# A new table of priorities, and a new split of sums between GpSimd and VectorE, in the two mixers of a hybrid decoder step

## The chip, the core and the metric

The program runs on one core of one Trainium2 chip. Its engines work side by side, each through its own instructions in their order: TensorE (PE in the profile) multiplies, VectorE (DVE), ScalarE (ACT) and GpSimd (POOL) do the elementwise work, SyncE (SP) issues the transfers. The metric is the device time of one execution in microseconds (us).

## The reference, cut to what matters

512 prompt tokens behind 16 learned ones, and 8 sample tokens, go through two layers. All is float32.

```python
x = x + 0.5 * _swiglu(_rmsnorm(x, norm_ffn1), ffn1_w_in, ffn1_w_out)
h, wkv, shift, conv = _mixer(_rmsnorm(x, norm_mix), ...)
x = x + h
x = x + 0.5 * _swiglu(_rmsnorm(x, norm_ffn2), ffn2_w_in, ffn2_w_out)

def _mixer(xn, ...):
    ps, pc, pg = split(xn @ w_in)                 # shifted, convolution and gate columns
    ...
    S = S * w_t + (S @ a_t) b_t + v_t k_t         # RWKV-7 state, token by token, 16 heads of 64
    y = S @ r_t
    ...
    m = sigmoid(gate_a) * y_a + sigmoid(gate_b) * (gb * conv(gc * hc))
    return m @ w_o, ...
```

## The kernel before, in words

The order on each engine is not the program's: class `Sched` records every operation (`add`), and `flush` runs a small model of the five engines and issues, on each engine in turn, the ready operation of lowest `prio`. A priority is the place in the program less `boost`. The model is flushed five times: for the FFN (swiglu) stretch of layer 0, its mixer, the FFN stretch between the layers, the mixer of layer 1, and the last FFN stretch. This case touches what the two mixers (`mixer`, called "mixer 0" and "mixer 1" here) hand to it.

A product of two float32 numbers is made of three products of rounded halves: a weight tile `raw` comes by a transfer of SP, ScalarE writes its upper half `hi`, VectorE the rest `lo` (`load_split`), and `mm3` issues for each 128 rows hi by xh, hi by xl, lo by xh, each for two halves of the columns (268, or 262 and 260 in layer 1). A projection (`proj`) is 48 such matmuls into one of two `acc` accumulators in PSUM. They are called column matmuls here.

A mixer has eight pairs of heads. Pair p goes through `stage_k(p)` (projections k and r, decay, key norm: `kq` is split into `kqh` and `kql` for the matmuls `wn`; the chunk matrix `mv`, its products `wg`; the inverse `Xinv` on GpSimd with `pr`), `stage_v(p)` (projection v, `wv`, `wg`, `wp`, and the bonus `bv`), `chain(p)` (11 chunks of 48 tokens that follow each other), `gnorm(p)` (group norm, with the split `yl`) and `stage_m(p)`. One step of a chain is PE, VectorE, ... in turn: `cq<-mv,sd` (PE), `rh` (VectorE), `cq<-cst,rh` (PE), `rd` (VectorE), `cq<-rd,Yd` (PE), `ud` (ScalarE), `cq<-GR,ud` (PE), `sx` and `P` (VectorE), `cq<-cst,sx` (PE), `sd` (VectorE). What PE has between these five matmuls are column matmuls of the next pairs and of `gated_parts`, the 40 gated projections with their elementwise work; `fill(p, i)` says how many of them are recorded at which place, by the list `gated`.

`sample` updates the state of the 8 sample rows in eight steps of 512 elements, on GpSimd and VectorE: `s1` (t<-s,VB), a sum, `sw` (s<-s,VB), `s2`, `s2a`, `s3`, `s3a`, `s4`, a sum. Its result `ys` goes into every column of the merged tile, so the first W_o product (`acc<-mh`) can't start without it.

The table `MIX` has one entry for each mixer: `boost` by stage (k, v, c chain, g gnorm, f gated parts, m, s sample, i inverse, w merge, e eviction of a projection, h weight loads), `gated`, `same` (how far ScalarE may put off an operation that needs another function table), and `vector`: the sums and products named there go to VectorE, the others to GpSimd:

```python
E = lambda n: V if n in opt['vector'] else G
...
E('kql').tensor_tensor(out=kql[:, :L], in0=kq[:, :L], in1=kqh[:, :L].bitcast(F32), op=ALU.subtract)
```

The model already counts one port that GpSimd and VectorE's operations with two SBUF inputs share (`o.port`, with `SHARE = 0.7`); that part is the same in both kernels. All recorded operations stand at line 273 of the profile, so rows are told apart by tile names.

Of the kernel before, what the change touches and what calls it, by code (L numbers as in the profile page):

```python
# [38 lines left out]
RW = C + D  # L39
NH = 16  # L40

MIX = [dict(boost={'k': 600, 'v': 2000, 'c': 2000, 'g': -1500, 'f': -1000, 'm': -1000, 's': -1000, 'i': 2000, 'w': -6000, 'e': 0, 'h': 0},
            ka=4, gated=[0, 2, 0, 0, 0, 1, 1, 1, 0, 0, 2, 1, 0, 1, 1, 2, 0, 1, 2, 1, 0, 0, 0, 1, 2, 2, 0, 0, 2, 1, 0, 0],
            same=3000, inv=(),
            vector=('bv', 'ka', 'kh', 'kql', 'kt', 'm', 'mb', 'rk', 'rnip', 'rt', 's1', 's3a', 'sl', 'u', 'yl', 'zg')),
       dict(boost={'k': 1500, 'v': -1000, 'c': 2000, 'g': 100, 'f': -3000, 'm': -50, 's': 1000, 'i': 1500, 'w': 50, 'e': -2000, 'h': -2000},
            ka=4, gated=[0, 3, 0, 0, 1, 0, 0, 1, 1, 0, 2, 2, 1, 0, 0, 1, 0, 0, 1, 4, 1, 0, 1, 0, 1, 1, 0, 1, 1, 1, 0, 0],
            same=0, inv=(),
            vector=('bv', 'kh', 'kql', 'kt', 'm', 'mb', 'rk', 'rt', 's3a', 'sl', 'u', 'yl', 'zg'))]
LATE = 4.0  # L50
SHARE = 0.7
FIRST = -300
# [307 lines left out]
class Build:  # L360
# [423 lines left out]
    def mixer(self, l, xh, xl, mD):  # L784
        tc, nc, io, cst, R = self.tc, self.nc, self.io, self.cst, self.R
        V, G, A, T, S = nc.vector, nc.gpsimd, nc.scalar, nc.tensor, nc.sync
        pc = lambda n, i: self.pcol(l, n, i)
        opt = MIX[l]
        nc.same = opt['same']
# [659 lines left out]
    def wo(self, l, X, mh, ml):  # L1449

        nc, n, ka = self.nc, self.n, MIX[l]['ka']
        for j in range(KD):
# [166 lines left out]
```

## Time and profile before

| | us |
|---|---|
| median of three runs | 2955.64 (2954.28 to 2958.29) |
| the profiled execution, its own time | 2957.18 |
| its span, first to last instruction | 2955.4 |
| PE busy | 2873.6 |
| VectorE busy | 2135.9 |
| ScalarE busy | 1362.6 |
| GpSimd busy | 587.7 |

The profile gives for each stretch of time how long each engine was busy, and the share of full speed that PE's clock was granted. A row of the timeline has the start, the length, the engine and operation, output<-inputs and shape; in brackets stands how long the engine sat idle before it, and what ended that.

### The profile page before, as it was taken

How to read it: one execution, taken by the hardware profiler on the slowest of the kernel's cores; microseconds unless marked ns; L12 is line 12 of the kernel's file. 1: busy time of each engine (PE TensorE's matmuls, PEld its weight loads, DVE VectorE, ACT ScalarE, POOL GpSimd, SP SyncE). 2: the span in 40 equal slices, each digit the busy share in tenths (PEclk: the TensorE clock that was granted, in tenths of full speed). 3: DMA queues.
4: the chain of work that ended last, by engine and by line, in shares of the span. 5: the costliest groups of instructions: out<-in, count | busy, mean ns of one | idle time of the engine just before them, and what ended most of it. 6: DMA issues, size and time to landing. Idle time of an engine off the chain costs nothing.

```text
span 2955.4 us, 57453 instructions
## 1 busy us (share of the span) xinstructions
PE 2873.6 (97%) x23026; PEld 2811.0 (95%) x23026; DVE 2135.9 (72%) x3995; ACT 1362.6 (46%) x2284; POOL 587.7 (20%) x1120
## 2 busy tenths in 40 slices
PE   8999999999999899999999999999999999999998
PEld 8999999999999899999999999999899998899997
DVE  8677767677776968676687766667766768687775
ACT  5444454344444245444454444535454442554444
POOL 1000026222342800000100001343430428100001
PEclk9999999999999989999999999999999999999999
DMA  3223323232323362323323333232232234623332
GB/s 133 93 96 98 112 87 92 74 86 83 87 64 99 130 207 87 104 90 104 108 71 101 100 94 116 90 96 78 62 84 75 62 103 139 214 79 108 96 102 80
DMA packets 219516, 294.22 MB, mean 100 GB/s; under 512 B 119824, under 2 KB 128784, under 8 KB 219248
## 3 DMA queue, kind: packets, MB, share of 16 engines
q1 hardware_dynamic: 219248, 290.54, 32.0%
q8 instruction: 181, 2.97, 0.4%
q14 instruction: 87, 0.71, 0.1%
HBM read 256.38 MB, written 34.10 MB: 98 GB/s over the span
## 4 chain that ended last, share of the span: by engine, by line
PE 86%; DVE 6%; ACT 2%; DMA 2%; issue 2%; POOL 1%; SPq 0%; DVEq 0%; ACTq 0%; POOLq 0%
PE acc L273 26%; PE a L273 17%; PE x L273 13%; PE y L273 7%; PE cq L273 5%; PE wg L273 3%; PE au L273 3%; PE z L273 3%; PE ag L273 3%; PE w L273 2%; DVE lo L273 2%; PE wp L273 2%; DMA raw<-in_f_in 1%; ACT hi L273 1%; POOL t L273 1%
## 5 line engine op out<-in xcount | busy, mean ns | idle before, releaser
L273 ACT ACTIVATE hi<-raw 128x1024 fp32r<-128x1024 f32 (+4 forms) x460 | 388.5, 845 | 488.6 <-PE acc L273 190.4
L273 DVE TENSOR_TENSOR lo<-raw,hi 128x1024 fp32r<-128x1024 f32 (+4 forms) x460 | 449.3, 978 | 58.0 <-ACT hi L273 52.2
L273 PE MATMUL acc<-xh,hi 128*128 128x268 f32 (+1 forms) x2112 | 481.3, 301 | 6.8 <-ACT sig L273 2.2
L273 PE MATMUL acc<-xh,lo 128*128 128x268 f32 (+1 forms) x2112 | 482.3, 301 | 5.5 <-DVE lo L273 5.4
L273 PE MATMUL acc<-xl,hi 128*128 128x268 f32 (+1 forms) x2112 | 478.2, 299 | 0.0
L273 PEld LDWEIGHTS acc<-xh,hi 128*128 128x128 f32 x2112 | 343.6, 192 | 12.5 <-ACT sig L273 3.3
L273 PEld LDWEIGHTS acc<-xh,lo 128*128 128x128 f32 x2112 | 343.6, 192 | 10.9 <-DVE lo L273 8.8
L273 PEld LDWEIGHTS acc<-xl,hi 128*128 128x128 f32 x2112 | 343.1, 191 | 1.1
L273 PE MATMUL a<-hh,lo 128*128 128x268 f32 (+1 forms) x1408 | 288.0, 285 | 0.9 <-DVE lo L273 0.9
L273 PE MATMUL a<-hl,hi 128*128 128x268 f32 (+1 forms) x1408 | 287.3, 285 | 0.0
L273 PE MATMUL a<-hh,hi 128*128 128x268 f32 (+1 forms) x1408 | 286.7, 285 | 0.0
L273 POOL MEMSET wide<- 128x104 f32 (+1 forms) x7 | 1.3, 188 | 1327.4 <-DVE s L273 945.8
L273 PE MATMUL x<-xh,hi 128*128 128x268 f32 (+1 forms) x864 | 247.3, 286 | 1.4 <-ACT sn L273 1.2
L273 PE MATMUL x<-xl,hi 128*128 128x268 f32 (+1 forms) x864 | 247.1, 286 | 0.0
L273 PE MATMUL x<-xh,lo 128*128 128x268 f32 (+1 forms) x864 | 246.9, 286 | 0.0
L273 ACT ACTIVATE hi<-s 128x1024 fp32r<-128x1024 f32 x144 | 152.0, 1057 | 185.8 <-DVE s L273 121.8
L273 PEld LDWEIGHTS a<-hh,lo 128*128 128x128 f32 x1408 | 219.6, 188 | 1.1 <-DVE lo L273 1.1
L273 PEld LDWEIGHTS a<-hl,hi 128*128 128x128 f32 x1408 | 218.6, 188 | 0.0
L273 PEld LDWEIGHTS a<-hh,hi 128*128 128x128 f32 x1408 | 218.6, 188 | 0.0
L273 DVE TENSOR_TENSOR lo<-s,hi 128x1024 fp32r<-128x1024 f32 x144 | 174.6, 1220 | 19.6 <-ACT hi L273 18.7
L273 POOL TENSOR_TENSOR pr<-Ta,Xinv 88x22 f32<-88x22 f32 (+16 forms) x368 | 149.6, 407 | 146.9 <-DMA Ta<-td 122.2
L273 DVE SCALAR_TENSOR_TENSOR X<-a,X 128x536 f32<-128x536 f32 (+1 forms) x160 | 113.0, 707 | 74.4 <-PE a L273 74.2
(570 smaller groups left out, 7204.3 us busy)
## 6 DMA issues: line engine op xcount, KB each, us to landing
raw<-in_f_in SPq DMA_DIRECT2D x176, 512.0 KB
raw<-in_w_in SPq DMA_DIRECT2D x132, 512.0 KB
raw<-in_f_out SPq DMA_DIRECT2D x128, 256.0 KB
raw<-in_f_out SPq DMA_DIRECT2D x32, 384.0 KB
raw<-in_w_o SPq DMA_DIRECT2D x32, 256.0 KB
XD<-X SPq DMA_DIRECT2D x16, 268.0 KB
s<-in_swkv SPq DMA_DIRECT2D x16, 256.0 KB
out_o_sswkv<-s SPq DMA_DIRECT2D x16, 256.0 KB
```

The source lines that it names most:

```text
L273: return getattr(getattr(self.nc, o.eng), o.fn)(*o.args, **o.kw)
```

## The change

The table gets other numbers, and nothing else in the file changes. In mixer 0 `bv`, `kql` and `s1` leave VectorE for GpSimd, and `sw` comes from GpSimd to VectorE; `gated` and six priorities differ. In mixer 1 `yl` leaves VectorE for GpSimd; `gated` and six priorities differ, and `same` goes from 0 to 3000. The number of projections, matmuls and transfers stays.

```diff
-MIX = [dict(boost={'k': 600, ..., 'm': -1000, 's': -1000, 'i': 2000, 'w': -6000, 'e': 0, 'h': 0},
+MIX = [dict(boost={'k': 874, ..., 'm': -940, 's': -860, 'i': 2131, 'w': -6000, 'e': 1682, 'h': 765},
...
-            vector=('bv', 'ka', 'kh', 'kql', 'kt', 'm', 'mb', 'rk', 'rnip', 'rt', 's1', 's3a', 'sl', 'u', 'yl', 'zg')),
+            vector=('ka', 'kh', 'kt', 'm', 'mb', 'rk', 'rnip', 'rt', 's3a', 'sl', 'sw', 'u', 'yl', 'zg')),
...
-            same=0, inv=(),
-            vector=('bv', 'kh', 'kql', 'kt', 'm', 'mb', 'rk', 'rt', 's3a', 'sl', 'u', 'yl', 'zg'))]
+            same=3000, inv=(),
+            vector=('bv', 'kh', 'kql', 'kt', 'm', 'mb', 'rk', 'rt', 's3a', 'sl', 'u', 'zg'))]
```

What that does to the order is shown at three places. The FFN stretches keep their order but for some 10 to 130 instructions of an engine right behind a mixer.

PE, mixer 0, the last pair (Yd1, GR of pair 7), its fifth step, before (`cq_6247`; acc_6395 and acc_6400 are two gated projections):

```order
L273 MATMUL acc_6395<-xh_775,hi_6393 128x268 x2
L273 MATMUL acc_6395<-xl_776,hi_6393 128x268 x2
L273 MATMUL cq_6241<-cst_69,sx_6245 128x128
L273 MATMUL acc_6400<-xh_775,hi_6398 128x268 x2
L273 MATMUL acc_6400<-xl_776,hi_6398 128x268 x2
L273 MATMUL cq_6247<-mv1_4732,sd_6246 128x160
L273 MATMUL cq_6247<-cst_69,rh_6248 96x128
L273 MATMUL cq_6247<-rd_6249,Yd1_4736 96x128
L273 MATMUL cq_6247<-GR_6000,ud_6250 128x128
L273 MATMUL cq_6247<-cst_69,sx_6251 128x128
L273 MATMUL acc_6395<-xh_775,lo_6394 128x268 x2
L273 MATMUL cq_6253<-mv1_4732,sd_6252 128x160
```

The same step on PE now, from its third matmul on:

```order
L273 MATMUL cq_6247<-rd_6249,Yd1_4736 96x128
L273 MATMUL acc_6383<-xl_784,hi_6381 128x268 x2
L273 MATMUL acc_6383<-xh_783,lo_6382 128x268 x2
L273 MATMUL acc_6383<-xh_785,hi_6381 128x268 x2
L273 MATMUL acc_6383<-xl_786,hi_6381 128x268
L273 MATMUL cq_6247<-GR_5993,ud_6250 128x128
L273 MATMUL acc_6383<-xl_786,hi_6381 128x268
L273 MATMUL acc_6383<-xh_785,lo_6382 128x268 x2
L273 MATMUL acc_6383<-xh_787,hi_6381 128x268 x2
L273 MATMUL acc_6383<-xl_788,hi_6381 128x268 x2
L273 MATMUL acc_6383<-xh_787,lo_6382 128x268
L273 MATMUL cq_6247<-cst_69,sx_6251 128x128
```

Before, the five matmuls of this step stood with nothing between them, and two other matmuls to the next step; now 49 stand under it.

GpSimd, mixer 0, in the inverse of pair 1 (`pr`, `Xinv`), before:

```order
L273 TENSOR_TENSOR pr_4868<-Ta_4866,Xinv_4867 88x68
L273 COPY NS_4723<-ps__5001 128x9
L273 TENSOR_TENSOR Xinv_4867<-Xinv_4867,pr_4868 88x4x17
L273 TENSOR_TENSOR pr_4868<-Ta_4866,Xinv_4867 88x64
L273 TENSOR_TENSOR Xinv_4867<-Xinv_4867,pr_4868 88x4x16
```

The same place now:

```order
L273 TENSOR_TENSOR pr_4863<-Ta_4861,Xinv_4862 88x68
L273 TENSOR_TENSOR Xinv_4862<-Xinv_4862,pr_4863 88x4x17
L273 COPY pe_5007<-pm_5006 128x11
L273 TENSOR_TENSOR pr_4863<-Ta_4861,Xinv_4862 88x64
L273 TENSOR_TENSOR kql_5010<-kq_5008,kqh_5009 128x528
L273 TENSOR_TENSOR Xinv_4862<-Xinv_4862,pr_4863 88x4x16
L273 TENSOR_TENSOR pr_4863<-Ta_4861,Xinv_4862 88x75
```

The split of pair 2's key squares now goes between two steps of pair 1's inverse.

VectorE, mixer 0, the first pairs (k, cum, pm and mv of pair 1; lo_4834 and now lo_4827 are weights of gated projections), before:

```order
L273 SCALAR_TENSOR_TENSOR k_4818<-ps__4823,par_68,t__4824 128x528
L273 MEMSET u_4779 128x2
L273 TENSOR_TENSOR hc_4778<-acc_4777,R_75 128x536
L273 SCALAR_TENSOR_TENSOR cum_4837<-cst_69,sig_4829 128x528
L273 MEMSET pm_4838 128x11
L273 TENSOR_TENSOR u_4779<-gc_4773,hc_4778 128x536
L273 TENSOR_TENSOR lo_4834<-raw_4832,hi_4833 128x1024
```

And now:

```order
L273 TENSOR_TENSOR GT_4784<-wg_4788,cst_69 96x3x48
L273 TENSOR_TENSOR GR_4785<-wg_4788,cst_69 96x3x112
L273 TENSOR_TENSOR GT_4784<-wg_4789,cst_69 96x2x48
L273 TENSOR_TENSOR GR_4785<-wg_4789,cst_69 96x2x112
L273 SCALAR_TENSOR_TENSOR k_4811<-ps__4816,par_68,t__4817 128x528
L273 MEMSET pm_4838 128x11
L273 TENSOR_TENSOR lo_4827<-raw_4825,hi_4826 128x1024
L273 SCALAR_TENSOR_TENSOR cum_4837<-cst_69,sig_4822 128x528
```

The weights `lo` stood behind an eviction, a scan and a product; they now stand ahead of the scan, behind the four evictions of `wg`.

## Rows read from the trace of the kernel before

**Rows 1.** The page: the span, and busy time, share and instructions of each engine.

```profile
span 2955.4 us, 57453 instructions
PE 2873.6 (97%) x23026; PEld 2811.0 (95%) x23026; DVE 2135.9 (72%) x3995; ACT 1362.6 (46%) x2284; POOL 587.7 (20%) x1120
```

**Rows 2.** Busy time by stretch (start:end, length, then PE, PEld, DVE, ACT, POOL with their instructions, the granted clock, DMA share and GB/s): mixer 0, the FFN stretch behind it, mixer 1.

```profile
390.00:1110.00 720.00, 696.59 (x5534) 669.25 (x5533) 525.69 (x1188) 322.17 (x602) 258.41 (x529) 0.98 0.34 101
1110.00:1849.00 739.00, 738.59 (x5978) 737.90 (x5977) 541.62 (x809) 350.11 (x529) 21.88 (x17) 1.00 0.30 97
1849.00:2585.00 736.00, 706.42 (x5611) 675.63 (x5610) 525.61 (x1181) 336.94 (x618) 275.53 (x547) 0.98 0.34 100
```

**Rows 3.** The same view of shorter stretches: three near the end of mixer 0, and the end of mixer 1.

```profile
990.00:1010.00 20.00, 17.58 (x120) 16.12 (x119) 18.00 (x37) 7.44 (x14) 17.63 (x16) 0.91 0.53 177
1010.00:1030.00 20.00, 17.67 (x133) 16.34 (x132) 18.75 (x34) 6.92 (x15) 16.66 (x13) 1.00 0.28 94
1030.00:1050.00 20.00, 16.68 (x91) 15.24 (x92) 13.53 (x34) 4.62 (x16) 2.29 (x3) 0.66 0.39 131
...
2420.00:2540.00 120.00, 108.71 (x817) 102.99 (x816) 98.64 (x187) 45.98 (x95) 74.50 (x60) 0.96 0.50 162
```

**Rows 4.** Timeline of PE near the end of mixer 0: the first transposes of `sample`, the fifth step of pair 7, the first W_o product.

```profile
948.65 0.60 PE L273 MATMUL ws<-cst,V 128*48 128x128 f32 x4
...
1029.19 0.43 PE L273 MATMUL cq<-mv,sd 128*128 128x160 f32 x2
1030.58 0.32 PE L273 MATMUL cq<-cst,rh 128*96 128x128 f32 x1 [0.96 <-DVE rh L273]
1032.06 0.74 PE L273 MATMUL cq<-rd,Yd 96*96 96x128 f32 x2 [1.16 <-DVE rd L273]
1033.22 0.79 PE L273 MATMUL cq<-GR,ud 96*128 96x128 f32 x2 [0.42 <-ACT ud L273]
1034.52 0.47 PE L273 MATMUL cq<-cst,sx 128*128 128x128 f32 x1 [0.50 <-DVE P L273]
1035.64 0.82 PE L273 MATMUL acc<-xh,lo 128*128 128x268 f32 x2 [0.66 <-DVE lo L273]
...
1055.29 0.49 PE L273 MATMUL acc<-mh,hi 128*128 128x268 f32 x2
```

**Rows 5.** Timeline of VectorE in mixer 0: the last step of pair 3 and the first of pair 4 (`sd`), two `lo` of equal size, the first step of pair 7, the first merged tile, the last step of pair 7.

```profile
778.25 0.34 DVE L273 SCALAR_TENSOR_TENSOR sd<-cq,pe,cr 128x128 f32<-128x128 f32 x1
791.57 0.35 DVE L273 SCALAR_TENSOR_TENSOR sd<-cq,pe,cr 128x128 f32<-128x128 f32 x1 [0.58 <-PE cq L273]
...
957.31 1.22 DVE L273 TENSOR_TENSOR lo<-raw,hi 128x1024 fp32r<-128x1024 f32 x1
...
1003.55 0.35 DVE L273 SCALAR_TENSOR_TENSOR sd<-cq,pe,cr 128x128 f32<-128x128 f32 x1 [0.31 <-PE cq L273]
...
1008.83 2.06 DVE L273 TENSOR_TENSOR lo<-raw,hi 128x1024 fp32r<-128x1024 f32 x1
...
1049.27 0.72 DVE L273 TENSOR_TENSOR ml<-mr,mh 128x536 fp32r<-128x536 f32 x1 [0.28 <-ACT mh L273]
...
1074.81 0.34 DVE L273 SCALAR_TENSOR_TENSOR sd<-cq,pe,cr 128x128 f32<-128x128 f32 x1
```

**Rows 6.** Timeline of GpSimd at the times of the two `lo` of rows 5.

```profile
959.47 1.28 POOL L273 TENSOR_TENSOR s<-s,VB 128x512 f32<-128x512 f32 x1 [2.22 <-DVE t L273]
...
1009.77 2.28 POOL L273 TENSOR_TENSOR s<-s,t 128x512 f32<-128x512 f32 x1
```

**Rows 7.** Groups of instructions in mixer 0 (shape and count, then busy us and mean ns of one, then idle time before them): `s1`, `kql` and `bv` on VectorE, `sw` on GpSimd.

```profile
L273 DVE TENSOR_TENSOR t<-s,VB 128x512 f32<-128x512 f32 x8 | 7.5, 942 | 0.0
L273 DVE TENSOR_TENSOR kql<-kq,kqh 128x528 fp32r<-128x528 f32 x8 | 5.6, 704 | 1.2 <-ACT kqh L273 1.1
L273 DVE TENSOR_TENSOR bv<-rs,v 128x528 f32<-128x528 f32 x8 | 5.6, 696 | 0.0
...
L273 POOL TENSOR_TENSOR s<-s,VB 128x512 f32<-128x512 f32 x8 | 11.4, 1426 | 3.5 <-DVE t L273 3.5
```

**Rows 8.** The same view of mixer 1: `yl` on VectorE, and `ka`, a product of 528 columns that stands on GpSimd there.

```profile
L273 DVE TENSOR_TENSOR yl<-P,yh 128x144 fp32r<-128x144 f32 x24 | 8.7, 362 | 2.1 <-ACT yh L273 1.6 <-PE w L273 0.4
L273 DVE TENSOR_TENSOR yl<-P,yh 128x96 fp32r<-128x96 f32 x8 | 2.9, 362 | 0.5 <-ACT yh L273 0.5
...
L273 POOL TENSOR_TENSOR ka<-k,a 128x528 f32<-128x528 f32 x8 | 10.5, 1317 | 26.0 <-PE wn L273 19.2 <-DVE kql L273 6.7
```

**Rows 9.** Timeline of PE: the largest wait at the start of mixer 0, the wait for `kql` of pair 2, the largest wait at the start of mixer 1.

```profile
444.45 0.82 PE L273 MATMUL acc<-xh,lo 128*128 128x268 f32 x2 [1.86 <-DVE lo L273]
...
489.34 0.52 PE L273 MATMUL wn<-kql,cr 128*128 128x264 f32 x2 [0.28 <-DVE kql L273]
...
1922.47 3.35 PE L273 MATMUL wg<-mv,BK 128*96 128x160 f32 x12 [3.43 <-DVE mv L273]
```

**Rows 10.** Timeline of VectorE at the start of mixer 0: a pair of evictions of `wg`, `k`, `lo`.

```profile
434.75 0.31 DVE L273 TENSOR_TENSOR GT<-wg,cst 96x144 f32<-96x144 f32 x1 [0.46 <-PE wg L273]
434.98 0.49 DVE L273 TENSOR_TENSOR GR<-wg,cst 96x336 f32<-96x336 f32 x1
...
438.84 0.77 DVE L273 SCALAR_TENSOR_TENSOR k<-ps__4823,par,t__4824 128x528 f32<-128x528 f32 x1 [0.53 <-ACT t__4824 L273]
...
443.18 1.22 DVE L273 TENSOR_TENSOR lo<-raw,hi 128x1024 fp32r<-128x1024 f32 x1
```

More of the change, by code (lines that the diff above doesn't have):

```diff
@@ L40 @@
 NH = 16
-MIX = [dict(boost={'k': 600, 'v': 2000, 'c': 2000, 'g': -1500, 'f': -1000, 'm': -1000, 's': -1000, 'i': 2000, 'w': -6000, 'e': 0, 'h': 0},
-            ka=4, gated=[0, 2, 0, 0, 0, 1, 1, 1, 0, 0, 2, 1, 0, 1, 1, 2, 0, 1, 2, 1, 0, 0, 0, 1, 2, 2, 0, 0, 2, 1, 0, 0],
+MIX = [dict(boost={'k': 874, 'v': 2000, 'c': 2000, 'g': -1500, 'f': -1000, 'm': -940, 's': -860, 'i': 2131, 'w': -6000, 'e': 1682, 'h': 765},
+            ka=4, gated=[0, 1, 0, 0, 0, 2, 0, 2, 0, 0, 1, 1, 0, 2, 2, 2, 1, 0, 2, 1, 0, 0, 0, 0, 1, 1, 0, 0, 3, 0, 1, 1],
             same=3000, inv=(),
-            vector=('bv', 'ka', 'kh', 'kql', 'kt', 'm', 'mb', 'rk', 'rnip', 'rt', 's1', 's3a', 'sl', 'u', 'yl', 'zg')),
-       dict(boost={'k': 1500, 'v': -1000, 'c': 2000, 'g': 100, 'f': -3000, 'm': -50, 's': 1000, 'i': 1500, 'w': 50, 'e': -2000, 'h': -2000},
-            ka=4, gated=[0, 3, 0, 0, 1, 0, 0, 1, 1, 0, 2, 2, 1, 0, 0, 1, 0, 0, 1, 4, 1, 0, 1, 0, 1, 1, 0, 1, 1, 1, 0, 0],
-            same=0, inv=(),
-            vector=('bv', 'kh', 'kql', 'kt', 'm', 'mb', 'rk', 'rt', 's3a', 'sl', 'u', 'yl', 'zg'))]
+            vector=('ka', 'kh', 'kt', 'm', 'mb', 'rk', 'rnip', 'rt', 's3a', 'sl', 'sw', 'u', 'yl', 'zg')),
+       dict(boost={'k': 1457, 'v': -1000, 'c': 2063, 'g': 100, 'f': -5869, 'm': -1268, 's': 1000, 'i': 1498, 'w': 50, 'e': -2663, 'h': -2000},
+            ka=4, gated=[0, 3, 0, 0, 1, 0, 0, 1, 1, 0, 2, 2, 1, 0, 0, 1, 0, 1, 1, 2, 1, 1, 1, 1, 1, 1, 1, 0, 0, 0, 1, 0],
+            same=3000, inv=(),
+            vector=('bv', 'kh', 'kql', 'kt', 'm', 'mb', 'rk', 'rt', 's3a', 'sl', 'u', 'zg'))]
 LATE = 4.0
```

## The prediction, made before the changed kernel was timed

> **What bounds the kernel now.** I read the busy times first. PE works 2873.6 of 2955.4 us [rows 1]; the number of matmuls is the same in both kernels, so only what PE loses can move: time in which it waits, and time at the lower clock level. The busy time by stretch says where. In the FFN stretch between the mixers PE loses 0.4 of 739 us, at clock 1.00; it also gives the price of a column matmul, 738.59 / 5978 = 0.1236 us. Mixer 0 has 23.4 us without work and a clock of 0.98 (of the levels 2.4 and 1.2 GHz, so 2% of 720 us is lost to slow work, some 14 us), mixer 1 has 29.6 us and again some 15 [rows 2]. About 82 us, 2.8% of the time, is all that any order could win. Two fifths of that lies in two stretches near the mixers' ends. The three stretches of 20 us from 990 to 1050 lose 8.1 us idle, and their clocks cost (0.09 + 0.00 + 0.34) x 20 = 8.6 us more; at the end of mixer 1, 11.3 us idle and 0.04 x 120 = 4.8 [rows 3]. In the first two of these stretches VectorE is busy 36.8 of 40 us and GpSimd 34.3: the sample update shares them with the last chains. In the third both have little to do, but PE, after its waits, works at a mean of 0.66. The timeline shows the hole that stands ahead of that. The fifth step of pair 7 runs with nothing between its five matmuls and waits 0.96, 1.16, 0.42 and 0.50 us for VectorE and ScalarE, and then 0.66 for a `lo` [rows 4]. So the question is whether the new order puts cover under the last chain without opening a hole elsewhere.
>
> **The change part by part.** The sum goes against the profiled execution's own 2957.2 us (span 2955.4, 1.8 around it); the median of the runs is 1.5 below that.
>
> (1) The last chain of mixer 0. Counted in the two orders, other matmuls under pair 7's eleven steps go from 384 to 450, and under the fifth step from 2 to 49. 66 x 0.1236 = 8.2 us of cover arrive there. They come from places where no chain runs: before, 76 stood between the last step of pair 3 and the first of pair 4, which is the 13.3 us between 778.25 and 791.57 in which no step ends, and 46 between pairs 4 and 5; now each chain starts before the one ahead of it ends. Pair 7's last ten steps took 1074.81 - 1003.55 = 71.3 us [rows 5]. The waits in the hole come to 3.0 us, and the clock behind them to 6.8 (0.34 x 20) [rows 3, 4]: 9.8 us is the most that this place gives. The other end: the first W_o matmul starts at 1055.29, and it needs `sample`, whose path ran from 948.65 to the first `ml` at 1049.27, written by 1050 [rows 4, 5]. That path is GpSimd's and VectorE's own and doesn't get shorter because PE is better fed. It starts 36 matmuls earlier in PE's order (4.4 us), so W_o could start at about 1045.6, 9.7 us earlier; but `s1` goes to GpSimd, where a product of this size takes 1.43 us against 0.94 [rows 7], and if all of 8 x 0.48 = 3.9 us lies on the path, 5.8 us earlier is all. I take 7.0, between 5.8 and 9.7; the range takes in 0. What is late next is the sample path, then.
>
> (2) Thin steps elsewhere. Steps with fewer than 30 matmuls of cover, without a chain's first and last: in mixer 0 six before and two now, in mixer 1 seven and three. Added up, the matmuls that lack to 30 go from 54 to 2 (28 of them already in part 1) and from 44 to 16: 52 x 0.1236 = 6.4 us if PE waited at each for all of it. It can be nothing where VectorE is early. I take a third, 2.0.
>
> (3) The start of mixer 1. PE waited 3.43 us for `mv` there [rows 9]. Between the projection it comes from and `wg`, 39 matmuls now stand where 17 stood: 22 x 0.1236 = 2.7 us. But a weight split `lo` of 1.22 us [rows 5] now stands ahead of `mv` on VectorE, and projection v waits for that `lo` itself. 0 to 2.7; I take 1.0.
>
> (4) The start of mixer 0. Before, a `lo` stood behind a scan and a product, and PE waited 1.86 us [rows 9]. Now it stands ahead of them but behind two pairs of `wg` evictions and `k`. By the rows 1.60 at most, 0.77 and 1.22 us, 3.6 in all [rows 10], against 12 matmuls (1.5 us) that PE has between `wg` and this `lo`: a wait of about 2 us again. I count 0; it can give back the 1.9.
>
> (5) The end of mixer 1. Cover under its last chain goes from 483 to 463 matmuls: up to 2.5 us worse, by a stretch that already loses 16. The thinnest step gets better (24 to 32). I take 1.0 against.
>
> (6) The sums that move. VectorE loses 8 x 0.704 + 8 x 0.696 = 11.2 us in mixer 0 and 32 x 0.362 = 11.6 in mixer 1 [rows 7, 8]. GpSimd gains 16 x 1.317 = 21.1 us by the row of `ka`, and 32 pieces that take between 0.36 (VectorE's price) and 1.317 us [rows 8]. On PE's path stands only `kql`, eight times: it comes (1.317 - 0.704) = 0.6 us later, plus what GpSimd has ahead of it, since it now goes between steps of the inverse. The new order has 15.1 matmuls between the two halves of `wn` on the mean where 6.8 stood, 1.0 us more cover; the one wait for `kql` before was 0.28 us [rows 9]. Cover and delay cancel: 0. `bv` and `yl` have a chain's length to come, and `bv` hides behind it. Whether VectorE is really relieved, the two `lo` of equal size show: 1.22 us while GpSimd idled (2.2 us without work ahead of 959.47), 2.06 us while GpSimd ran its sums [rows 5, 6]. So up to 0.84 us comes back for each sum on GpSimd that meets one of these. 22.8 us of relief against as many as 48 sums: I take 0, and both signs go into the range.
>
> The Trainium skill (SBUF — State Buffer, "Who interferes with whom") says why: a VectorE instruction with two SBUF inputs and a GpSimd instruction that reads SBUF take one port pair for the whole instruction, and the second blocks. The trace agrees (1.22 against 2.06 us). By that page a sum that costs 0.70 us on VectorE and 1.32 on GpSimd holds the pair longer after the move, so the move relieves VectorE of less than 0.70, or of nothing; this is rival A below.
>
> (7) Nothing else has a price: transfers are as many and stand in SP's queue in another order, with the DMA at 0.34 of its time in the mixers [rows 2]; ScalarE has 322 and 337 us of work in 720 and 736 us [rows 2], which hides the new `same`.
>
> Sum: -7.0 - 2.0 - 1.0 + 1.0 = -9.0; 2957.2 - 9.0 = 2948.2 profiled, so 2946.6 for the median.
>
> **The rivals.** *A, GpSimd gives the time back (slower).* Its place is mixer 0's VectorE queue. If each of the 16 moved sums of 1.32 us makes a `lo` or a chain's neighbour wait the 0.84 us of the two rows, and the sample path, which uses the same engines, grows by 3.9 us beyond what part 1 counts (half a microsecond for each of its eight steps), it comes to -9.0 + 13.4 + 3.9 = +8.3, 2963.9. For it: in the sample stretch both engines are over 85% busy, and `bv` of the last pairs lands in it. Against it: GpSimd has 461 of 720 us free in mixer 0 [rows 2], so most of the 16 meet idle neighbours. It decides once more than half of them hit a `lo` that PE waits for next. *B, holes only move (no change).* Cover that is put under pair 7 is missing at another place that the counts of matmuls don't show, since they don't know when VectorE delivers; part 4 is an example. Then only parts 2 and 3 are left at half: -1.5 and +1.0, 2955.1. *C, the chains even out everywhere.* Parts 1 and 2 at their upper ends, 9.7 + 6.4, and 1.9 of part 4: -18, 2937.6. For it: the cover of all eight chains of mixer 0 was between 374 and 448 and is between 387 and 450.
>
> **How the numbers follow.** The forecast 0.45, A 0.19, B 0.26, C 0.10. A measurement of this kernel can tell 0.2%, 5.9 us, from no change: faster is under 2949.7, slower over 2961.5. The forecast's own range, with part 1 between 5.8 and 9.7 and part 5 up to 2.5, reaches 2943 to 2950, and 0.05 of it lies within the 0.2%. So faster 0.40 + 0.10 = 0.50, same 0.26 + 0.05 = 0.31, slower 0.19. The range that leaves out 2 in 10 goes from 2937 (C inside) to 2962 (A's half above).
>
> **What would show it.** Part 1: between 970 and 1050 fewer than four waits over 0.4 us at pair 7's steps, the stretch of half clock gone, and the first W_o matmul 5 to 10 us earlier against the mixer's start. Sample path: `ml` at most 1 us ahead of W_o's start. Part 3: a wait of 2 to 3 us, split in two, at the first `wg` of pair 1 in mixer 1. Part 4: a wait for `lo` of about 2 us near the first `wg`. Part 6: `kql` waits under 0.3 us; GpSimd about 21 us and 10 to 40 us busier in the two mixers; the mean of a `lo` of 1024 columns unchanged. Rival A would show as longer `lo` and `u`, rival B as new waits in mixer stretches that were clean. The prediction is wrong if a single wait at a new place drops the clock for several stretches, which the counts can't foresee.

## The result, and the profile after

The changed kernel takes 2929.52 us (median of 4 runs, 2925.43 to 2931.06), the kernel before 2955.29 beside it. The ratio is 0.9909, interval 0.9892 to 0.9926: 26 us faster, where 9 were forecast and the range ended at 2937. The direction was right, the size was not. The profiled execution is the fastest of the four, 2925.43 us with a span of 2923.7, and its mean granted clock is 0.994 where the other three have 0.992 (0.002 of 2924 us is 5.8), so the two traces differ by 31.7 us, some 6 more than the medians. Each trace below is one execution: 31 executions of the kernel before took 2951.74 to 2968.26 us, at granted clocks between 0.991 and 0.986, so a few us of any difference between two traces can be their own.

The page of the changed kernel answers to [rows 1]:

```profile
span 2923.7 us, 57448 instructions
PE 2853.2 (98%) x23026; PEld 2790.6 (95%) x23026; DVE 2132.2 (73%) x3947; ACT 1365.4 (47%) x2284; POOL 629.3 (22%) x1168
```

To see where the time went, both traces are cut at the same work: from VectorE's first eviction in a mixer to its first addition of a W_o product into X. Busy time by stretch (columns as in rows 2), the kernel before: mixer 0, the stretch between the mixers, mixer 1.

```profile
401.30:1092.50 691.20, 669.58 (x5343) 642.85 (x5342) 507.19 (x1158) 308.69 (x580) 250.75 (x521) 0.98 0.34 97
1092.50:1860.30 767.80, 765.60 (x6166) 764.30 (x6167) 560.61 (x844) 363.47 (x549) 29.59 (x24) 1.00 0.31 101
1860.30:2558.60 698.30, 670.83 (x5342) 640.98 (x5340) 500.46 (x1138) 318.16 (x588) 263.71 (x537) 0.98 0.33 96
```

The changed kernel, the same three, and behind them the stretches that answer to [rows 3]:

```profile
400.70:1080.70 680.00, 660.91 (x5343) 635.36 (x5341) 509.85 (x1141) 312.87 (x582) 268.98 (x537) 1.00 0.35 99
1080.70:1848.10 767.40, 763.89 (x6166) 762.05 (x6167) 560.03 (x844) 364.41 (x549) 30.18 (x24) 1.00 0.32 101
1848.10:2527.00 678.90, 662.55 (x5342) 633.17 (x5341) 492.18 (x1106) 316.41 (x586) 287.64 (x569) 0.99 0.34 99
990.00:1010.00 20.00, 15.54 (x110) 13.62 (x108) 20.00 (x28) 8.77 (x14) 15.21 (x11) 1.00 0.38 127
1010.00:1030.00 20.00, 17.52 (x130) 16.16 (x131) 20.00 (x35) 6.50 (x11) 10.72 (x11) 1.00 0.42 138
1030.00:1050.00 20.00, 19.63 (x162) 19.22 (x162) 15.28 (x44) 9.64 (x26) 0.38 (x2) 1.00 0.70 224
2406.00:2526.00 120.00, 111.12 (x852) 105.75 (x851) 93.98 (x177) 50.70 (x96) 69.83 (x60) 0.97 0.53 176
```

Mixer 0 is 11.2 us shorter, mixer 1 is 19.4, and the stretch between them the same. PE has the same matmuls in each, so a shorter mixer is made of two things: PE's idle time (length less busy time), and the time at the lower clock, of which half is lost. Idle time went from 21.6 to 19.1 us in mixer 0 and from 27.5 to 16.4 in mixer 1. The stretches that the trace's clock shows at 1.2 GHz add up to 23.9 us before and 3.4 after in mixer 0, 23.9 and 6.8 in mixer 1. So mixer 0 should have won 2.5 + 10.2 = 12.7, mixer 1 11.1 + 8.5 = 19.6: the account closes within 1.5 us. In these two traces 13.6 us of it are waits and 18.7 are the clock; between the medians, which differ by some 6 us less, the clock's share is some 13 by an estimate: all of the 6 taken from the clock, as 0.994 beside 0.992 suggests.

PE's longest waits now (timeline; what ended each wait is in brackets): the start of mixer 0, the steps beside `sample`, the first W_o product, and in mixer 1 the first `wg` of pair 1 and the end.

```profile
418.50 0.56 PE L273 MATMUL acc<-xh,hi 128*128 128x268 f32 x2 [1.56 <-ACT sig L273]
438.72 0.52 PE L273 MATMUL acc<-xh,lo 128*128 128x268 f32 x2 [0.74 <-DVE lo L273]
...
996.46 0.32 PE L273 MATMUL cq<-cst,rh 128*96 128x128 f32 x1 [1.24 <-DVE rh L273]
1001.00 0.51 PE L273 MATMUL acc<-xh,lo 128*128 128x268 f32 x2 [1.17 <-DVE lo L273]
1010.28 0.33 PE L273 MATMUL cq<-cst,sx 128*128 128x128 f32 x1 [1.41 <-DVE P L273]
1016.23 0.46 PE L273 MATMUL cq<-rd,Yd 96*96 96x128 f32 x2 [0.81 <-DVE rd L273]
...
1045.13 0.49 PE L273 MATMUL acc<-mh,hi 128*128 128x268 f32 x2
...
1909.42 0.46 PE L273 MATMUL wg<-mv,BK 128*96 128x160 f32 x2
...
2450.68 0.51 PE L273 MATMUL acc<-xh,lo 128*128 128x262 f32 x2 [2.02 <-DVE lo L273]
2454.48 0.90 PE L273 MATMUL cq<-mv,sd 128*128 128x160 f32 x2 [2.21 <-DVE sd L273]
```

The hole of [rows 4] is gone, but the waits in the sample stretch are not: PE idles 6.9 us between 990 and 1030, where it idled 4.8. They now stand 4.5 to 9.3 us apart, and the clock stays at 1.00 through all three stretches, where it was 0.91, 1.00 and 0.66 [rows 3]. The wait of 3.43 us for `mv` [rows 9] is gone from mixer 1 without a remainder. What is left stands at its end: 2.02 and 2.21 us, with 6.8 us at half clock from 2453.2 on, inside the second of them.

### The profile page after: what moved, and what is told of

Same layout as the page of the kernel before. It is cut to its first block, busy times and chain, and to the rows that moved or that the text cites. A ratio compares the mean times of both kernels' runs of the same rounds, so it can differ in the third digit from the quotient of the medians.

```text
span 2923.7 us, 57448 instructions
## 1 busy us (share of the span) xinstructions
PE 2853.2 (98%) x23026; PEld 2790.6 (95%) x23026; DVE 2132.2 (73%) x3947; ACT 1365.4 (47%) x2284; POOL 629.3 (22%) x1168
## 4 chain that ended last, share of the span: by engine, by line
PE 88%; DVE 6%; ACT 2%; issue 2%; DMA 1%; POOL 1%; SPq 0%; DVEq 0%; ACTq 0%; POOLq 0%
PE acc L273 26%; PE a L273 18%; PE x L273 14%; PE y L273 7%; PE cq L273 5%; PE z L273 3%; PE wg L273 3%; PE au L273 3%; PE ag L273 3%; PE w L273 2%; PE wp L273 2%; DVE lo L273 1%; DVE s L273 1%; DMA raw<-in_f_in 1%; ACT hi L273 1%
## 5 line engine op out<-in xcount | busy, mean ns | idle before, releaser
L273 DVE TENSOR_TENSOR lo<-raw,hi 128x1024 fp32r<-128x1024 f32 (+4 forms) x460 | 456.4, 993 | 65.9 <-ACT hi L273 54.4
L273 PE MATMUL y<-xh,hi 128*128 128x268 f32 (+1 forms) x576 | 164.6, 286 | 2.1 <-ACT hi L273 2.1
```

Source lines behind the costliest of these rows:

```text
L273: return getattr(getattr(self.nc, o.eng), o.fn)(*o.args, **o.kw)
```

## The experiments

The first four take the change apart by mixer, and into order and split. All their stretches are cut at the same work as above. Each ratio is against the kernel before.

**One mixer's table at a time** (`m0_new`, `m1_new`).

```diff
-MIX = [dict(<mixer 0, new>), dict(<mixer 1, new>)]
+MIX = [dict(<mixer 0, new>), dict(<mixer 1, before>)]    # m0_new
+MIX = [dict(<mixer 0, before>), dict(<mixer 1, new>)]    # m1_new
```

Expected of the first:

> Mixer 0 has the new table, mixer 1 the old one. Theory (the new order removes PE's waits in each mixer by itself, and the half-clock time behind them): mixer 0's share alone, some 10 to 13 us faster than the kernel before (2942 to 2945); mixer 1 keeps its 3.43 us wait for mv, its idle time of about 29.6 us and its half-clock stretches. Rival (the mixers hang together, by what one leaves over for the next): mixer 1 changes too, by over 5 us.

Expected of the second:

> Mixer 1 has the new table, mixer 0 the old one. Theory: 17 to 21 us faster than the kernel before (2934 to 2938), twice what mixer 0 gives, with PE idle in mixer 1 down from 29.6 us to about 18.5 and the clock there up from 0.98 to 0.99; mixer 0 keeps its hole of 13.7 us at half clock near 1031. Rival (a chance hit of the whole, not of mixer 1): under 10 us.

Measured: 0.9977 (0.9964 to 0.9990) and 0.9942 (0.9929 to 0.9955), some 7 and 17 us. The two mixers of `m0_new`, then of `m1_new`, in the view by stretch:

```profile
399.70:1080.10 680.40, 660.65 (x5343) 635.24 (x5341) 510.07 (x1142) 312.60 (x582) 268.85 (x537) 1.00 0.35 99
1848.20:2548.60 700.40, 670.27 (x5342) 638.52 (x5340) 501.96 (x1139) 315.64 (x585) 257.41 (x537) 0.99 0.34 96
```

```profile
399.70:1090.30 690.60, 668.63 (x5343) 640.78 (x5341) 506.89 (x1158) 308.30 (x580) 250.60 (x521) 0.99 0.35 98
1859.60:2540.60 681.00, 663.25 (x5342) 634.58 (x5340) 494.59 (x1107) 313.36 (x584) 281.88 (x569) 0.99 0.35 98
```

Each mixer gains by its own table (10.8 and 17.3 us in the traces) and the other stays within 2.1 us of what it was. The timed 7 us of `m0_new` is under the 10 to 13 expected, and less than the 10.8 of its mixer 0; the place is right.

**Order and split apart.** The recorded engine sets the order; the operation is then issued at that place on another engine.

```diff
+MOVE = [{'bv': 'vector', 'kql': 'vector', 's1': 'vector', 'sw': 'gpsimd'}, {'yl': 'vector'}]
-        return getattr(getattr(self.nc, o.eng), o.fn)(*o.args, **o.kw)
+        return getattr(getattr(self.nc, o.real), o.fn)(*o.args, **o.kw)
```

`old_order_new_split` has the old table and the opposite moves. Expected:

> The order of every operation is the changed kernel's, but the moved sums (bv, kql, s1, sw in mixer 0, yl in mixer 1) are issued, at the same places of that order, on the engine that had them before. Theory (the order brings the gain, the split of sums little): within 5 us of the changed kernel, 2925 to 2935. Rival (the split relieves VectorE by 22.8 us on the queue that PE waits for): over 8 us slower than the changed kernel, 2938 or more, with new waits for lo and for the chains' rh, rd and sd.

> The order of every operation is the kernel before's, but the moved sums are issued, at the same places of that order, on the engines that have them in the changed kernel. Theory: within 5 us of the kernel before (2950 to 2960), or slower, since the old order has no room ahead of kql. Rival (the split relieves VectorE): over 8 us faster, 2947 or less.

Measured: 0.9904 (0.9889 to 0.9919), the changed kernel's own ratio, and 1.0026 (1.0012 to 1.0041), slower. The mixers of the new order with the old split, then of the old order with the new split:

```profile
402.80:1080.90 678.10, 658.50 (x5343) 634.80 (x5342) 510.14 (x1158) 312.59 (x582) 245.35 (x521) 1.00 0.35 100
1848.00:2525.30 677.30, 662.11 (x5342) 632.85 (x5341) 498.57 (x1138) 316.23 (x586) 266.68 (x537) 0.99 0.35 99
```

```profile
400.90:1103.80 702.90, 673.04 (x5344) 643.56 (x5342) 504.26 (x1143) 308.78 (x580) 265.79 (x537) 0.98 0.34 96
1872.90:2572.00 699.10, 670.19 (x5342) 640.55 (x5340) 492.49 (x1107) 318.28 (x588) 278.91 (x569) 0.99 0.34 96
```

So all of the gain, as far as the runs can tell, is the order. In it the split costs 1.9 and 1.6 us in the traces, which the runs can't tell from nothing. In the old order the same split costs 11.7 us in mixer 0 by one trace each (8.3 of them are PE's idle time, 29.9 us where 21.6 stood), and 7.7 us of the whole by the ratio (3.6 to 12). It is paid where `sample` and the last chains share the two engines, and at `kql`, as PE's timeline of `old_order_new_split` shows:

```profile
490.32 0.51 PE L274 MATMUL wn<-kql,cr 128*128 128x264 f32 x2 [0.89 <-POOL kql L274]
...
984.93 0.54 PE L274 MATMUL cq<-mv,sd 128*128 128x160 f32 x2 [1.19 <-DVE sd L274]
...
996.83 0.46 PE L274 MATMUL cq<-rd,Yd 96*96 96x128 f32 x2 [1.56 <-DVE rd L274]
...
1004.89 0.32 PE L274 MATMUL cq<-cst,rh 128*96 128x128 f32 x1 [2.14 <-DVE rh L274]
...
1038.00 0.33 PE L274 MATMUL cq<-cst,sx 128*128 128x128 f32 x1 [1.93 <-DVE P L274]
```

The Trainium skill (SBUF — State Buffer, "Who interferes with whom") states that the order of issue, and not the kind of operation, decides who is blocked at the shared port pair. The two prices of one split, 11.7 and at most 1.9 us, fit that but don't prove it: what part is the port and what part GpSimd's longer sums stays open.

**Mixer 1's numbers, one part back at a time.** Mixer 0 is new in all five, and everything not named is the changed kernel's; the fifth goes the other way, from the old mixer 1.

```diff
-       dict(boost={'k': 1457, ..., 'c': 2063, ..., 'f': -5869, 'm': -1268, ..., 'i': 1498, ..., 'e': -2663, ...},
+       dict(boost={'k': 1500, ..., 'c': 2000, ..., 'f': -3000, 'm': -50, ..., 'i': 1500, ..., 'e': -2000, ...},   # m1_old_boost
-            ka=4, gated=[..., 0, 1, 1, 2, 1, 1, 1, 1, 1, 1, 1, 0, 0, 0, 1, 0],
+            ka=4, gated=[..., 0, 0, 1, 4, 1, 0, 1, 0, 1, 1, 0, 1, 1, 1, 0, 0],   # m1_old_gated
-            same=3000, inv=(),
+            same=0, inv=(),   # m1_same0
-            vector=(..., 'u', 'zg'))]
+            vector=(..., 'u', 'yl', 'zg'))]   # m1_yl_v
```

`m1_same_only` is the old table of mixer 1 with `same=3000`. Expected of the five, in this order:

> The changed kernel, but mixer 1's six priorities (k, c, f, m, i, e) are the old ones; gated, same and the place of yl stay new. Mixer 1's stretch took 698.4 us in the kernel before and 678.9 in the changed one. Theory (the numbers are fitted to one another, and no single one carries the gain): it goes to 685 to 700, 8 to 20 us slower than the changed kernel. Rival (one part carries it, and it is not this one): 677 to 682.

> The changed kernel, but mixer 1's list gated is the old one. Theory (fitted to one another): mixer 1's stretch 685 to 700 us, 6 to 20 us slower than the changed kernel, the new waits in its second half, where the two lists differ. Rival (another part carries the gain): 677 to 682.

> The changed kernel, but ScalarE may not put off an operation that needs another function table in mixer 1 (same back to 0). Theory (fitted to one another): mixer 1's stretch 683 to 700 us. Rival (same itself carries the gain, since ScalarE is late with hi, yh and ud in the kernel before, 3.4, 1.9 and 1.1 us of PE's waits): all of it lost, 696 to 700, with these waits back; if it does nothing, 677 to 682.

> The changed kernel, but yl stays on VectorE in mixer 1, and the order is made with it there. Theory (fitted to one another; at the same places of the order yl's engine made 1.6 us): mixer 1's stretch 683 to 700 us, from the other order alone. Rival (GpSimd's relief of VectorE carries the gain): 690 or more, with waits for lo, rh, rd and sd where VectorE is late; if neither, 677 to 682.

> Mixer 0 has the new table; mixer 1 the old one, with same at 3000 alone. With the old table behind the new mixer 0, mixer 1's stretch took 700.4 us. In this kernel's order 20 other matmuls of the stage stand between pair 1's projection and its first wg, as in the changed kernel, where 4 stood before. Theory (same takes away the wait of 3.4 us for mv and nothing else; the rest of the gain needs the other numbers too): 693 to 698 us, the wait for mv gone, the waits at the end of mixer 1 still there. Rival (same carries most of the 18 us): 680 to 687.

Mixer 1 in the view by stretch, one row for each, in the same order:

```profile
1849.70:2542.10 692.40, 666.48 (x5342) 634.38 (x5341) 499.96 (x1107) 314.86 (x586) 287.33 (x569) 1.00 0.34 97
```

```profile
1849.80:2546.80 697.00, 672.96 (x5342) 641.28 (x5340) 492.37 (x1106) 321.02 (x590) 283.68 (x569) 0.98 0.34 96
```

```profile
1848.80:2552.80 704.00, 672.69 (x5343) 641.39 (x5341) 495.73 (x1107) 311.89 (x582) 280.90 (x569) 0.98 0.34 95
```

```profile
1850.70:2551.30 700.60, 673.46 (x5342) 643.61 (x5340) 504.44 (x1138) 317.04 (x586) 258.22 (x537) 0.98 0.34 96
```

```profile
1852.00:2558.30 706.30, 675.04 (x5342) 643.53 (x5340) 504.00 (x1138) 321.22 (x589) 264.58 (x537) 0.98 0.34 95
```

In the table, "half clock" is the time at 1.2 GHz within mixer 1, and "lacking" the prediction's own count: the matmuls that thin steps lack to 30.

| kernel | ratio (interval) | mixer 1 | idle | half clock | lacking |
|---|---|---|---|---|---|
| changed | 0.9909 (0.9892 to 0.9926) | 678.9 | 16.4 | 6.8 | 16 |
| m1_new | 0.9942 (0.9929 to 0.9955) | 681.0 | 17.7 | 10.2 | 29 |
| m1_old_boost | 0.9944 (0.9930 to 0.9959) | 692.4 | 25.9 | 6.8 | 37 |
| m1_old_gated | 0.9969 (0.9958 to 0.9981) | 697.0 | 24.0 | 27.3 | 66 |
| before | 1 | 698.3 | 27.5 | 23.9 | 44 |
| m0_new | 0.9977 (0.9964 to 0.9990) | 700.4 | 30.1 | 17.1 | 37 |
| m1_yl_v | 0.9993 (0.9982 to 1.0005) | 700.6 | 27.1 | 34.1 | 70 |
| m1_same0 | 0.9980 (0.9971 to 0.9989) | 704.0 | 31.3 | 30.7 | 40 |
| m1_same_only | 0.9979 (0.9965 to 0.9994) | 706.3 | 31.3 | 34.1 | 46 |

Any one of the four parts put back loses 13.5, 18.1, 25.1 or 21.7 us of mixer 1 (old priorities, old `gated`, `same` 0, `yl` on VectorE): 78 us together, of a gain of 19.4. By the ratios, which time the whole kernel, they lose some 10, 18, 21 and 25 us, so this doesn't hang on single executions. Each of the four parts is needed, then: the numbers fit one another. Of the parts alone on the old table, only `same` was run. The first two losses lie in the expected ranges; `m1_same0` (704.0) and `m1_yl_v` (700.6) came out above the 683 to 700 of their theory. `yl` shows best that it is the order: at the changed kernel's places its engine is worth 1.6 us, but the order that the model makes with it on VectorE is 21.7 us longer.

`m1_same_only` is a miss of both its theories: with `same` alone the wait for `mv` is gone, as in the changed kernel, but nothing is won. Its ratio is that of `m0_new` (0.9979 and 0.9977). Its trace has a mixer 1 that is 5.9 us longer, with a new wait of 3.02 us and twice the time at half clock; as that execution took 2959.55 us where the median is 2955.0, the 5.9 us can be its own. And `m1_same0` has more than the wait for `mv` back: a wait of 3.20 us for VectorE at 2471.84, near the end of mixer 1, is new in it. PE's timeline of `m1_same0`, with the wait for `mv`, and then of `m1_same_only`, with its new one:

```profile
1911.06 1.35 PE L273 MATMUL wg<-mv,BK 128*96 128x160 f32 x4 [3.46 <-DVE mv L273]
```

```profile
2187.41 0.46 PE L273 MATMUL cq<-rd,Yd 96*96 96x128 f32 x2 [3.02 <-DVE ps__23987 L273]
```

In all nine rows the stretch, less the idle time and half of the half clock, lies between 656 and 664 us, while the stretch itself goes from 679 to 706. So idle time and clock are nearly all that tells these kernels apart.

**The price of a wait.** The changed kernel, with waits made in the clean stretch between the mixers: GpSimd copies an input of the last matmul and one of the next onto themselves, and PE waits for that.

```diff
+HOLES = set(range(600, 5400, 800))        # holes_long: 6 holes of 6 copies
+HOLES = set(range(600, 5400, 267))        # holes_short: 18 of 2 copies
+HOLES = {a + b for a in range(600, 5400, 800) for b in (0, 16, 32)}    # holes_bunch: 6 x 3 of 2 copies
...
+            if self.seen in HOLES:
+                for ap in [self.last] + [rhs] * 5:          # * 1 in the other two
+                    self.nc.gpsimd.tensor_copy(out=ap, in_=ap.bitcast(F32))
```

Expected:

> The changed kernel with six holes made on PE in the FFN stretch between the mixers, where it has no waits and a clock of 1.00: at six places, 800 matmuls apart, GpSimd copies the inputs of the next matmul onto themselves six times. Each hole should be some 3 us long, 15 to 20 us in all. Theory (a long wait costs its length and a stretch at half clock behind it, as at the 3.43 us wait of the kernel before, with 3.4 us at half clock): the FFN stretch of 767.4 us grows by more than the idle time, by 6 times 1.7 us or more; 25 to 35 us. Rival (the clock follows other things, and the gain of the changed kernel is waits alone): it grows by the idle time and no more.

> The same with eighteen holes of two copies, 267 matmuls (some 33 us) apart, about 1 us each. Theory (short waits far from one another leave the clock up, as the seven waits of 0.8 to 1.5 us between 953 and 1017 in the changed kernel did): the FFN stretch grows by the idle time alone, no stretch at half clock. Rival (each wait costs the clock): 18 stretches of 3.4 us at half clock, 30 us above the idle time.

> The same eighteen holes of two copies, in six groups of three, 16 matmuls (some 2 us) apart within a group. Theory (waits that stand close together cost the clock like one long wait, as the six between 1027.9 and 1035.6 in the kernel before, with 13.7 us at half clock behind them): more than the idle time by 10 us or more, with stretches at half clock behind most groups. Rival (only the length of a single wait counts): the same growth as with the eighteen spread out.

Measured: 1.0006 (0.9995 to 1.0017), 1.0010 (1.0000 to 1.0020) and 0.9998 (0.9988 to 1.0009), so 26 to 30 us above the changed kernel. The stretch between the mixers, in this order:

```profile
1080.80:1880.50 799.70, 774.93 (x6166) 771.68 (x6167) 562.77 (x843) 364.86 (x549) 48.77 (x60) 0.99 0.31 96
```

```profile
1084.10:1883.30 799.20, 772.71 (x6166) 767.22 (x6167) 564.45 (x844) 366.26 (x549) 51.23 (x60) 0.99 0.31 96
```

```profile
1080.60:1881.50 800.90, 776.14 (x6166) 770.35 (x6167) 563.68 (x843) 364.97 (x549) 48.49 (x60) 0.99 0.31 96
```

Beside 767.4 us with 3.5 idle, the six long holes (2.8 to 4.7 us) add 21.3 us of idle time and 32.3 of length; at five of the six the clock falls to half, for 23.9 us in all, worth 11.9. The theory holds there.

The eighteen short ones (0.9 to 2.3) add 23.0 and 31.8, with two stretches of 3.4 at half clock: fewer than the rival's eighteen, more than the theory's none. Both stand at holes that came out longer than the 1 us meant, of 2.25 and 2.10 us; two others of 2.13 and 2.21 left the clock at 1.00, and so did all fourteen of 0.88 to 1.84. For waits of the length that it named, in this stretch, the theory holds. PE's timeline of `holes_short`, the longest of them:

```profile
1435.64 0.39 PE L282 MATMUL x<-xl,hi 128*128 128x268 f32 x1 [2.25 <-POOL xl L280]
```

In bunches they add 21.3 and 33.5, with half clock at two groups of the six, 13.7 us, not "behind most"; the longest waits of these two groups are 1.78 and 1.85 us, so close to others such waits did bring the clock down, where in `holes_short` none of that length did. At the very start of the stretch, ahead of the first hole, stand another 3.4 and 6.8 us at half clock in these two; without their half the lengths grow by 30.1 us each. So bunches are not dearer on the whole than the same holes spread out, and this part of the theory falls. Between 2 and 4 us of the last two kernels' growth is seen neither as idle time nor at half clock; its cause stays open. Taken together a microsecond of wait costs 1.3 to 1.5 us.

## Why the prediction was right in mixer 0 and wrong in mixer 1

*Part 1 (the last chain of mixer 0), right in size, in part by luck.* W_o starts 644.4 us behind the mixer's start, where it was 654.0 (1055.29 - 401.3): 9.6 us earlier, against 5.8 to 9.7 allowed. The terms were others. The path of `sample` starts 536.1 us behind the mixer's start, where it was 547.4: 11.2 us earlier, not 4.4. It takes 3.5 us longer (104.1 for 100.6), near the 3.9 feared. And it doesn't hold W_o, as the text had it: the first `ml` ends 3.5 us ahead of W_o, which PE reaches without a wait. PE's and VectorE's timelines, the first transposes of `sample`, the first `sd` of pair 7, the first `ml`, the last `sd` of pair 7:

```profile
936.83 0.60 PE L273 MATMUL ws<-cst,V 128*48 128x128 f32 x4
...
985.44 0.60 DVE L273 SCALAR_TENSOR_TENSOR sd<-cq,pe,cr 128x128 f32<-128x128 f32 x2
...
1040.93 0.72 DVE L273 TENSOR_TENSOR ml<-mr,mh 128x536 fp32r<-128x536 f32 x1 [0.38 <-ACT mh L273]
...
1059.82 0.35 DVE L273 SCALAR_TENSOR_TENSOR sd<-cq,pe,cr 128x128 f32<-128x128 f32 x1 [0.59 <-PE cq L273]
```

The second of the two `sd` at 985.44 is pair 7's. Its last ten steps take 74.1 us now, where they took 71.3 [rows 5]: the last chain is no shorter under its new cover, it starts 17 us earlier. "Fewer than four waits over 0.4 us" is wrong too: seven stand between 970 and 1050, four of them in pair 7's own matmuls. What went is the half clock.

*Part 2 (thin steps), right in sign, far too small for mixer 1.* Of the nine kernels in the table the two with the fewest lacking matmuls, 16 and 29, have the two short mixers; the other seven (37 to 70) don't follow the count. A third of 28 x 0.1236 us, 1.2, was set against a difference of 19.4.

*Part 3 (the start of mixer 1), mis-sized.* The wait of 3.43 us went whole, and 3.4 us at half clock behind it: 5.1, where 2.7 was the limit and 1.0 taken. In its cause part 7 erred: the new `same` was given no price, but it alone brings these matmuls in front of `wg`. Between the last matmul of the projection r of pair 1 and its first `wg`, 17 others stand in every order with 0 and 39 in every order with 3000, whatever the rest of the table. They cover 2.7 of the 3.43 us; the rest is that `mv` itself comes earlier, since from that matmul to `wg` it took 6.0 us before and 5.5 now. What on VectorE's side let it stays open.

*Part 4 (the start of mixer 0), right in its sum, 0.* Waits of 1.56 us for `sig` and 0.74 for `lo`, where about 2 was forecast, stand where one of 1.86 was, and 3.4 us at half clock stand in both traces; nothing won.

*Part 5 (the end of mixer 1), the step that failed in sign.* 463 matmuls of cover for 483 were to cost 1.0 us. In the last 120 us PE idles 8.9 where it idled 11.3 [rows 3], and the last ten steps of pair 7 take 74.7 us instead of 80.7. How much cover stands under a chain as a whole doesn't say where in it PE waits.

*Part 6 (the split), right in its sum, 0, and wrong in one sign.* GpSimd is busy 18.2 and 23.9 us longer. `kql` and `bv` cost 1.43 and 1.47 us there (1.317 was taken), the larger `yl` 0.68. `kql` costs PE one wait of 0.2 us. The mean of a `lo` of 1024 columns was to stay; it rose from 1251 to 1324 ns in mixer 0. At the changed kernel's order it is 1271 with the old split, so 53 of the 73 ns come with the split, 65 x 0.053 = 3.4 us. And it isn't `lo` alone: in that order the moved sums take 10.6 us off VectorE in mixer 0 (5.8 for `bv`, 5.8 for `kql`, 7.2 for `s1`, less 8.2 for `sw`), but its busy time falls by 0.3 us, from 510.14 to 509.85; in mixer 1 11.3 us of `yl` make it fall by 6.4. So in mixer 0 VectorE was relieved of next to nothing, as the prediction's text on rival A held possible. In the old order the same move cost PE 8.3 us of idle time, in the new one next to nothing. Groups of instructions in mixer 0 (shape, count, busy us and mean ns), first `lo` with the new order and the old split, then the changed kernel, then its mixer 1:

```profile
L274 DVE TENSOR_TENSOR lo<-raw,hi 128x1024 fp32r<-128x1024 f32 x65 | 82.5, 1271 | 6.3 <-PE acc L274 3.1 <-ACT hi L274 2.7
```

```profile
L273 DVE TENSOR_TENSOR lo<-raw,hi 128x1024 fp32r<-128x1024 f32 x65 | 86.0, 1324 | 7.0 <-ACT hi L273 3.5 <-PE acc L273 3.1
...
L273 POOL TENSOR_TENSOR bv<-rs,v 128x528 f32<-128x528 f32 x8 | 11.7, 1466 | 11.7 <-DVE gs L273 11.7
L273 POOL TENSOR_TENSOR kql<-kq,kqh 128x528 fp32r<-128x528 f32 x8 | 11.4, 1429 | 4.4 <-ACT kqh L273 2.8 <-DVE mv L273 1.6
```

```profile
L273 POOL TENSOR_TENSOR yl<-P,yh 128x144 fp32r<-128x144 f32 x24 | 16.3, 682 | 46.5 <-ACT yh L273 21.0 <-PE acc L273 9.2 <-ACT rs L273 7.8
```

*The rivals.* A is real, with its place as told: +11.7 us in mixer 0, beside the +17.3 that it was given (13.4 + 3.9), when the split meets the old order, 7.7 by the ratio. The new order avoids it. B (holes only move) is what happened to mixer 0's waits, 21.6 to 19.1 us, but it took moved waits to cost as much as before, and where they stand now the clock stayed up. C (everything evens out) came nearest, 2937.6, but it looked for the gain in mixer 0.

*The step that failed* is the sum for mixer 1, and *the term that was mis-sized* in both mixers is the clock. Mixer 1 was made of -1.0, +1.0 and some -1 of part 2, from three places picked out of the order; it came out 19.4 us shorter, since all of its waits changed, 11.1 us in idle time, and the clock with them. Mixer 0 was to give some 8 us, and gave 11.2. The first paragraph counted some 29 us of clock in the mixers; in the sum it was priced at one hole, at most 6.8. In the two traces it gave 18.7 us, and by the estimate above some 13 between the medians.

**What stays open.** That mixer 1's gain is the order, and that none of its four parts can be left out, is shown. Whether two of them would do, or other numbers in their place, is not. Whether this table is more than a good one among many, is not; the runs tried six others in mixer 1, and the nearest was 13.5 us longer.

## What to carry to other kernels

Where an engine is busy 97% of the time and its clock falls at waits, as here, add to each wait what the clock costs (here 0.3 to 0.5 us for each 1 us in a clean stretch, and in the mixers about as much as the waits themselves, 18.7 us beside 13.6 in the traces, some 13 between the medians by estimate). A table that a scheduler turns into an order can't be priced number by number: one part back cost between 13.5 and 25.1 us, of a gain of 19.4. And before an engine swap is credited or blamed, run it at fixed places of the order: the same split cost 11.7 us in one order (7.7 by the ratio) and next to nothing in the other. A trace is one execution: read a gain from the medians, and the place of it from the trace.

## What was not expected of the hardware

Six waits of 0.8 to 1.5 us between 977 and 1017 left the changed kernel's clock at 1.00, while the five of 0.4 to 1.2 within 6 us [rows 4] stand in a stretch at 0.66. (There the half clock begins at 1031.2, behind the first of the five and a wait of 1.18 us at 1027.90; the other four end in it, so it stands not only behind the hole, as the prediction put it.) Yet neither length nor distance settles it: of the six long holes one of 2.79 us left the clock at 1.00 and another of 2.79 did not, and only two of the six bunches brought it down. PE's timeline of `holes_long`, the longest hole and the one without loss, and the granted clock behind each (13 matmuls in 3 us at 0.50, 26 at 1.00):

```profile
1160.06 0.59 PE L282 MATMUL y<-xl,hi 128*128 128x268 f32 x1 [4.70 <-POOL xl L280]
...
1263.32 0.39 PE L282 MATMUL z<-xh,hi 128*128 128x268 f32 x1 [2.79 <-POOL xh L280]
```

```profile
1160.00:1163.00 3.00, 2.94 (x13) 2.94 (x14) 0.00 (x0) 0.40 (x1) 0.01 (x1) 0.50 0.06 23
...
1264.00:1267.00 3.00, 3.00 (x26) 3.00 (x25) 1.64 (x3) 1.03 (x2) 0.00 (x0) 1.00 0.00 0
```
